# Second blocks of at most 64 tokens on column halves of the matmul array, in a hybrid decoder layer with a mixture of experts

## The chip, the cores and the metric

The kernel runs on one core of a Trainium2 chip. The metric is the device time of one execution in microseconds (us), the median of several runs. TensorE (PE) multiplies, VectorE (DVE) and ScalarE (ACT) do element-wise work, GpSimd (POOL) issues the gathers and scatters here, and SyncE (SP) issues the loads and stores. [...]

## What is computed

One decoder layer on 1024 tokens of width 1024 in float32: token mixing, then a mixture of experts, each with a residual and a layer norm. The change lies in the experts. A router picks for each token one of 4 groups and in it 2 of 8 experts, so 2048 assignments fall on 32 experts. Cut to that part, the reference is:

```python
def expert_block(args):
    xblk, e = args
    gu = xblk @ w_up[e]                      # 1024 -> 2 x 512
    return (jax.nn.silu(gu[:, :MOE_HIDDEN]) * gu[:, MOE_HIDDEN:]) @ w_down[e]   # 512 -> 1024
...
y = (yb.astype(jnp.float32) * pad_w[:, None]).astype(h.dtype)
out = jnp.zeros((t, d), h.dtype).at[pad_tok].add(y)
```

Each expert has its own `w_up` (4 MB) and `w_down` (2 MB); all 32 are read once.

## The kernel before

The mixing and the router take the first half of the time. The rest is the expert stage: 32 positions `e`, one expert each, in a loop written out at build time. The first four positions (`FIXED`) are experts 0 to 3. The others are sorted on the chip by their number of tokens and dealt out by a table (`place`, `reorder`): the largest four go to positions 5, 12, 19 and 26, the fifth to position 7. Those five (`BIG`) and the fixed four make up `TWO`, the positions that may have a second block of 128 tokens; anything beyond goes through a loop at the end that is skipped when nothing is left.

For each position a register `N[e]` holds (tokens + 127) / 16, rounded down. Branches on it choose the form. With N over 11 (more than 64 tokens) the first block runs whole; with N of 10 or 11 it is `parts(2)`, with at most 32 tokens `parts(4)`. In the whole form (`up_whole`, `down_whole`) the stationary operand is 128x128, the tokens of a block. In the parts (`up_parts`, `down_parts`) it is 64 or 32 columns wide, and the 2 or 4 matmuls that belong together write to different partitions of one PSUM bank, each with another slice of the weights. A float32 matmul leaves two records in the trace. With N over 15 (more than 128 tokens) there is a second block, which runs whole whatever its size: its up part goes to the PSUM tile `pup2` (named `ov` in the trace), `hidden` and `turn_hidden` make `eh2` of it, its down part goes to `pup2` again, and `result` weighs it into `yo2`, which a scatter adds to `xad` in DRAM. The scatters and gathers are cut to 16, 32, 48, 64 or 128 rows by `by_size`.

The weights come in tiles of 1 MB (two k of 128 rows) in the order `SEQ`: four up tiles of position e, then two down tiles of position e-1. `eload` issues a load on SP as soon as the code has released a tile, and the 19 tiles of the rings (`ring`, `pring` and the reused `more`, `gs`, `vn`, `y0a`, `y0b`, `y1a`, `uu`) are reused in turn. On each engine the order is the program's: for position e the first four k of up, the hidden layer of e-1 turned, the last four k of up, the tokens of e+1 turned, then down and finish of e-1. Every scatter to `xad` waits for the one before it to land, and at the end `xad` is read back for the last layer norm.

A branch on `N[e]` stands in the program of every engine that holds the register: TensorE, VectorE, and for positions of `TWO` ScalarE and GpSimd too, also where the engine has no work inside.

Of the kernel before, what the change touches and what calls it, by code (L numbers as in the profile page):

```python
# [59 lines left out]
def tile_hybrid_moe_layer(  # L60
# [1051 lines left out]
    ext = [pe.tile([P, 8, P], F32, name=f"ext{i}") for i in range(3)]  # L1112
# [4 lines left out]
    yo2 = pe.tile([P, 1024], F32, name="yo2")  # L1117
    N = {}
    TWO = [*range(FIXED), *BIG]
# [96 lines left out]
    def by_size(n, f, base=0):  # L1216
        with tc.If(n > base + 9) as some:
            with tc.If(n > base + 11) as many:
                f(slice(0, P))
            with many.Else():  # L1220
                with tc.If(n > base + 10) as more:
                    f(slice(0, 64))
                with more.Else():
                    f(slice(0, 48))
        with some.Else():
            with tc.If(n > base + 8) as more:
                f(slice(0, 32))
            with more.Else():
                f(slice(0, 16))
# [21 lines left out]
    eh, eh2 = (p4.tile([P, 4, P], F32, name=n) for n in ("eh", "eh2"))  # L1251
    wr, wr2 = ([p4.tile([P, 1], F32, name=f"{n}{i}") for i in range(m)] for n, m in (("wr", 2), ("wq", 3)))
# [46 lines left out]
    pup, pup2, pdn = (ps4.tile([P, 2, 512], F32, name=t) for t in ("up", "ov", "dn"))  # L1299
# [38 lines left out]
    def gate_up(w, m, j):  # L1338
        return w.rearrange("p (a b n) -> p a b n", a=2, b=m)[:, :, j]

    def up_whole(p, x, ks, w):
        for k in ks:
            for h in range(2):
                PE.matmul(p[:, h], x[:, k], gate_up(w[k], 2, h), start=k == 0, stop=k == 7)  # L1344

    def up_parts(m, p, x, ks, w):
        r = P // m
        o = p[:, 0].rearrange("p (a n) -> p a n", a=2)
        if m == 4:
            o = o[:, :, 0:256:2]  # L1350
        for k in ks:
            for j in range(m):
                c = gate_up(w[k], 2, j // 2)[:, :, j % 2:256:2] if m == 4 else gate_up(w[k], m, j)
                PE.matmul(o[j * r:(j + 1) * r], x[:, k, 0:r], c, start=k == 0, stop=k == 7)

    def down_whole(p, h, ks, w):
        for k in ks:
            for n in range(2):
                PE.matmul(p[:, n], h[:, k - 8], w[k][:, COLS[n]], start=k == 8, stop=k == 11)  # L1359

    def down_parts(m, p, h, ks, w):
        r, c = P // m, 4 // m
        for k in ks:
            j, i = divmod(k - 8, c)
            for q in range(m):
                PE.matmul(p[q * r:(q + 1) * r, 0, 0:D // m], h[:, i, j * r:(j + 1) * r],
                          w[k][:, q * (D // m):(q + 1) * (D // m)], start=k == 8, stop=k == 11)

    def by_parts(n, whole, parts):
        with tc.If(n > 9) as some:  # L1370
            with tc.If(n > 11) as many:
                whole()
            with many.Else():
                parts(2)
        with some.Else():
            parts(4)

    def up(e, ks, w):
        b = e % 2

        def whole():
            up_whole(pup, ext[b], ks, w)
            if e in TWO:
                with tc.If(N[e] > 15):
                    up_whole(pup2, ext[2], ks, w)

        by_parts(N[e], whole, lambda m: up_parts(m, pup, ext[b], ks, w))

    def down(e, ks, w):
        p = pd(e)  # L1390

        def whole():
            down_whole(p, eh, ks, w)
            if e in TWO:
                with tc.If(N[e] > 15):
                    down_whole(pup2, eh2, ks, w)

        by_parts(N[e], whole, lambda m: down_parts(m, p, eh, ks, w))

    def pd(e):  # L1400
        return pup2 if e == NE - 1 and e not in TWO else pdn
# [17 lines left out]
    def result(yo, p, w, m=1):  # L1419
        r, c = P // m, D // max(m, 2)  # L1420
        for n in range(max(m, 2)):
            rows, src = slice(0, r), (p[n * r:(n + 1) * r, 0, 0:c] if m > 1 else p[:, n])
            V.scalar_tensor_tensor(yo[rows, n * c:(n + 1) * c], src, w[rows], g2p[rows, n * c:(n + 1) * c],  # L1423
                                   op0=OP.mult, op1=OP.mult)

    def scatter(yo, tcol, rows):
        G.indirect_dma_start(out=xad, out_offset=bass.IndirectOffsetOnAxis(ap=tcol[rows], axis=0),  # L1427
                             in_=yo[rows], in_offset=None, bounds_check=T + P - 1, oob_is_err=True,
                             compute_op=OP.add)
# [17 lines left out]

    def finish_second(e):
        if e in TWO:
            with tc.If(N[e] > 15):  # L1450
                result(yo2, pup2, wr2[TWO.index(e) % 3])
                by_size(N[e], lambda rows: scatter(yo2, tokp[:, 1, e:e + 1], rows), 8)

    l2 = []
# [31 lines left out]
    def last_of(e):  # L1486
        down(e, range(8, 12), weights_of(e, range(8, 12)))
        release(e, range(8, 12))
        finish(e)
        finish_second(e)  # L1490

    for e in range(NE):
        up(e, range(4), weights_of(e, range(4)))
        release(e, range(4))
        if e == 0:
            reorder()
            ordered.append(True)
            while unused and len(RAW) < len(SEQ):
                eload()
        if e + 1 < NE:  # L1500
            count_all(e + 1)
            for x in (e + 1, e + 2):
                if x < NE and x == e + 1 + (x - 1 not in TWO):
                    gather_second(x)
        gather_weight(e, 0)
        if e:
            turn_hidden(act, eh)
            turn_hidden_second(e - 1)
        up(e, range(4, 8), weights_of(e, range(4, 8)))
        release(e, range(4, 8))  # L1510
        hidden(act, pup)
        hidden_second(e)
        turn_first(e + 1)
        if e:
            last_of(e - 1)
        if e + 1 < NE:
            turn_second(e + 1)
# [7 lines left out]
    with tc.If(most > 0):  # L1525
        free = list(unused)
        for e in range(NE):
            done = 1 + (e in TWO)
            ne = count(nbl, e, None, 8)
            with tc.If(ne > done):  # L1530
                x = e if e < FIXED else count(ordp, e, None, NE - 1)
                with tc.For_i(done, ne, 1) as j:
# [7 lines left out]
                    w = {}  # L1540
# [100 lines left out]
```

## Time and profile before

| | us |
|---|---|
| median of 3 runs | 1169.26 (1168.99 to 1174.07) |
| profiled execution | 1171.18 |
| its span, first to last instruction | 1169.3 |
| TensorE busy in the span | 1038.5 (89%) |
| VectorE, ScalarE, GpSimd busy | 553.8, 292.7, 358.9 |

The span is what the trace shows of the profiled execution; 1.9 us of its time lie around it. A busy TensorE is an account of issued matmuls, whose ends are modelled; it says nothing of how full the array is. The expert stage lies between about 570 and 1125 us of the span. In that stage the shares over the whole span don't help, since the stage has a stretch for each position with other sizes; it is read by stretches, by the waits in a stretch and by the order in time.

### The profile page before, as it was taken

The numbers are of one execution on the slowest core, as the hardware profiler recorded it, in microseconds if no ns is written. First come the engines' busy times: TensorE is split into PE (matmuls) and PEld (weight loads), VectorE is DVE, ScalarE is ACT, GpSimd is POOL, SyncE is SP. The second block draws the span as 40 slices with busy tenths as digits, with TensorE's granted clock in tenths as the row PEclk, the third lists the DMA queues.
The fourth block names the chain that finished last, engine by engine and source line by source line (L and its number), as shares of the span: only waits on it lengthen the run. The fifth ranks groups of instructions, "written<-read, shape, count | busy, mean of one in ns | idle before, by whom it ended". The sixth has DMA issues, their size and how long they took to land.

```text
span 1169.3 us, 16712 instructions
## 1 busy us (share of the span) xinstructions
PE 1038.5 (89%) x5758; PEld 687.5 (59%) x5758; DVE 553.8 (47%) x1018; ACT 292.7 (25%) x440; POOL 358.9 (31%) x271
## 2 busy tenths in 40 slices
PE   4999999899999989998678999899999999899920
PEld 3778888788788767777433454454444544454510
DVE  6858975737664489999511211130223113211338
ACT  3363326643224442221210110010011101110113
POOL 2325543262211236543412211231134113301225
PEclk9899999999999999999798999999999999899975
DMA  9954454444212325414999989999999999999964
GB/s 277 247 168 145 131 182 140 142 144 144 91 51 59 144 88 221 164 68 187 371 361 345 393 338 323 381 394 412 386 377 380 412 389 373 390 416 394 387 222 179
DMA packets 93631, 304.50 MB, mean 260 GB/s; under 512 B 14769, under 2 KB 42073, under 8 KB 68909
## 3 DMA queue, kind: packets, MB, share of 16 engines
q1 hardware_dynamic: 83900, 275.52, 63.4%
q0 software_dynamic: 8368, 22.90, 7.3%
q10 hardware_dynamic: 1216, 4.21, 0.9%
q8 instruction: 83, 1.36, 0.5%
q14 instruction: 64, 0.52, 0.1%
HBM read 281.09 MB, written 22.88 MB: 260 GB/s over the span
## 4 chain that ended last, share of the span: by engine, by line
PE 27%; DMA 25%; issue 25%; DVE 16%; ACT 3%; POOLq 1%; POOL 1%; SPq 1%; DVEq 0%; ACTq 0%
DMA xad<-yo,tokp 19%; DMA wr<-wd,aidp 4%; PE sm L302 4%; PE acc L623 3%; PE acc L625 3%; PE acc L624 3%; PE acc L621 2%; PE acc L619 2%; PE acc L620 2%; DVE y1a L234 1%; DMA wd<-w 1%; DVE pc L1022 1%; DVE Fg L886 1%; DMA xad<-Vv 1%; SPq L103 1%
## 5 line engine op out<-in xcount | busy, mean ns | idle before, releaser
L1406 DVE TENSOR_TENSOR act<-up,act 128x512 f32<-128x512 f32 x32 | 22.1, 692 | 299.7 <-ACT act L1405 244.3
L1427 POOL DMA_INDIRECT xad<-yo,tokp x36 | 52.9, 1470 | 231.7 <-DVE yo L1423 106.1
L1423 DVE SCALAR_TENSOR_TENSOR yo<-dn,wr,g2p 32x256 f32<-32x256 f32 (+2 forms) x94 | 52.1, 563 | 126.9 <-PE ov L1359 39.0
L1412 ACT ACTIVATE eh<-tp 128x512 f32<-128x512 f32 x36 | 21.1, 596 | 315.5 <-PE tp L1411 274.8
L623 PE MATMUL acc<-whi,hTh 128*128 128x512 f32 x192 | 83.1, 433 | 0.0
L1212 POOL DMA_INDIRECT KS<-h2d,tokp x32 | 30.6, 958 | 164.0 <-PE tp L1319 155.1
L166 ACT ACTIVATE whi<-wr 128x1024 fp32r<-128x1024 f32 (+1 forms) x44 | 44.9, 1021 | 128.1 <-PE acc L625 67.9
L625 PE MATMUL acc<-whi,hTl 128*128 128x512 f32 x192 | 76.0, 396 | 0.0
L624 PE MATMUL acc<-wlo,hTh 128*128 128x512 f32 x192 | 75.4, 393 | 0.0
L167 POOL TENSOR_TENSOR wlo<-wr,whi 128x1024 fp32r<-128x1024 f32 (+1 forms) x15 | 35.8, 2385 | 119.9 <-ACT whi L166 108.3
L302 PEld LDWEIGHTS sm<-QP,KS 128*128 128x128 f32 x448 | 58.2, 192 | 7.3 <-issue 3.3
L619 PE MATMUL acc<-hTh,whi 128*128 128x512 f32 x144 | 59.3, 411 | 0.0
L302 PE MATMUL sm<-QP,KS 128*128 128x64 f32 x448 | 56.1, 269 | 2.6 <-DVE KS L315 1.6
L1344 PE MATMUL up<-pring,ext 128*128 128x512 f32 x128 | 56.7, 593 | 1.6 <-DVE yo L1423 1.6
L621 PE MATMUL acc<-hTh,wlo 128*128 128x512 f32 x144 | 56.9, 395 | 0.5 <-DVE wlo L167 0.3
L881 PE MATMUL pa<-wh,yl 128*128 128x512 f32 (+1 forms) x128 | 51.8, 405 | 5.5 <-DVE yl L865 5.5
L620 PE MATMUL acc<-hTl,whi 128*128 128x512 f32 x144 | 56.7, 393 | 0.0
L880 PE MATMUL pa<-wl,yh 128*128 128x512 f32 (+1 forms) x128 | 51.3, 401 | 4.7 <-DVE wl L1052 4.7
L879 PE MATMUL pa<-wh,yh 128*128 128x512 f32 (+1 forms) x128 | 53.4, 417 | 1.5 <-ACT wh L1051 0.9
L1405 ACT ACTIVATE act<-up 128x512 f32<-128x512 f32 x32 | 19.1, 597 | 135.2 <-PE ov L1344 52.3
L443 POOL TENSOR_TENSOR vec<-vec,y1a 128x1024 f32<-128x1024 f32 x14 | 35.4, 2527 | 55.2 <-ACT y1a L442 55.2
L167 DVE TENSOR_TENSOR wlo<-wr,whi 128x1024 fp32r<-128x1024 f32 (+1 forms) x29 | 38.4, 1324 | 22.6 <-ACT whi L166 21.9
(476 smaller groups left out, 2243.2 us busy)
## 6 DMA issues: line engine op xcount, KB each, us to landing
pring<-in_w_up SPq DMA_DIRECT2D x52, 1024.0 KB, 20.5
pring<-in_w_down SPq DMA_DIRECT2D x28, 1024.0 KB, 8.5
ring<-in_w_up SPq DMA_DIRECT2D x28, 1024.0 KB, 16.4
wr<-in_w_in SPq DMA_DIRECT2D x44, 512.0 KB, 6.0
y1a<-in_w_ada SPq DMA_DIRECT2D x32, 512.0 KB, 4.0
ring<-in_w_down SPq DMA_DIRECT2D x12, 1024.0 KB, 20.4
y0a<-in_w_up SPq DMA_DIRECT2D x8, 1024.0 KB, 15.1
y0b<-in_w_up SPq DMA_DIRECT2D x8, 1024.0 KB, 24.3
```

The costliest lines, as they stand in the source:

```text
L167: (G if u % 3 == 2 and u > W8 else V).tensor_tensor(lo, w, hi, op=OP.subtract)
L302: PE.matmul(p[:, hd], chd(KS)[:, c4, hd], chd(QP)[:, c4, hd].rearrange("p (b two i) -> p b two i", two=2, i=h)[:, :, 1, :], start=True, st ...
L619: PE.matmul(a[i], hi[:, j, sl], hTh[k], start=st, stop=False)
L620: PE.matmul(a[i], hi[:, j, sl], hTl[k], start=False, stop=False)
L621: PE.matmul(a[i], lo[:, j, sl], hTh[k], start=False, stop=sp)
L623: PE.matmul(a[i], hTh[k][:, sl], hi[:, j], start=st, stop=False)
L624: PE.matmul(a[i], hTh[k][:, sl], lo[:, j], start=False, stop=False)
L625: PE.matmul(a[i], hTl[k][:, sl], hi[:, j], start=False, stop=sp)
L879: PE.matmul(p, yh[:, k], wh[k][:, sl], start=k == 0, stop=False)
L1344: PE.matmul(p[:, h], x[:, k], gate_up(w[k], 2, h), start=k == 0, stop=k == 7)
L1423: V.scalar_tensor_tensor(yo[rows, n * c:(n + 1) * c], src, w[rows], g2p[rows, n * c:(n + 1) * c], op0=OP.mult, op1=OP.mult)
L1427: G.indirect_dma_start(out=xad, out_offset=bass.IndirectOffsetOnAxis(ap=tcol[rows], axis=0), in_=yo[rows], in_offset=None, bounds_check=T ...
```

## The change

Where a position has a second block (N over 15), its size is looked at too. With N over 19 (more than 64 tokens in the second block) all stays as it was. Otherwise its up and down matmuls use the form `parts(2)`, 64 stationary columns and two column halves, and `result` reads the halves from one bank. `hidden`, `turn_hidden`, gather and scatter are unchanged. The finish of a second block now has two branches, one for `result` and one for the scatter.

```diff
+    def second_by_size(n, whole, halved):
+        with tc.If(n > 15):
+            with tc.If(n > 19) as many:
+                whole()
+            with many.Else():
+                halved()
...
             if e in TWO:
-                with tc.If(N[e] > 15):
-                    up_whole(pup2, ext[2], ks, w)
+                second_by_size(N[e], lambda: up_whole(pup2, ext[2], ks, w),
+                               lambda: up_parts(2, pup2, ext[2], ks, w))
...
             if e in TWO:
-                with tc.If(N[e] > 15):
-                    down_whole(pup2, eh2, ks, w)
+                second_by_size(N[e], lambda: down_whole(pup2, eh2, ks, w),
+                               lambda: down_parts(2, pup2, eh2, ks, w))
...
     def finish_second(e):
         if e in TWO:
+            second_by_size(N[e], lambda: result(yo2, pup2, wr2[TWO.index(e) % 3]),
+                           lambda: result(yo2, pup2, wr2[TWO.index(e) % 3], 2))
             with tc.If(N[e] > 15):
-                result(yo2, pup2, wr2[TWO.index(e) % 3])
                 by_size(N[e], lambda rows: scatter(yo2, tokp[:, 1, e:e + 1], rows), 8)
```

The first place is TensorE at position 26, the last four k of the up part (`ov` is the second block's tile, `ext_4022` its turned tokens, `y0b` and `y1a` the weight tiles; lines with - are of before, with + of after, and the line numbers of after are higher by up to 8).

```order
 L1344 MATMUL up<-y0b,ext_4020 128x512 x4
 L1344 MATMUL up<-y1a,ext_4020 128x512 x4
-L1384 COMPARE_AND_BRANCH
+L1379 COMPARE_AND_BRANCH
+L1380 COMPARE_AND_BRANCH
 L1344 MATMUL ov<-y0b,ext_4022 128x512 x4
 L1344 MATMUL ov<-y1a,ext_4022 128x512 x4
-L1384 UNCONDITIONAL_BRANCH x2
+L1380 UNCONDITIONAL_BRANCH
+L1354 MATMUL ov<-y0b,ext_4022 64x512 x4
+L1354 MATMUL ov<-y1a,ext_4022 64x512 x4
```

One more comparison stands ahead of the second block, and a second body with 64 columns stands behind the whole one; the matmuls of the first block and their order are untouched. TensorE's listing has 3981 rows before and 4152 after.

The second place is VectorE at the finish of the same position, before (`wq_4238` holds the weights of the second block's tokens, `yo_4039` is `yo2`):

```order
1554 L1217 UNCONDITIONAL_BRANCH
1555 L1450 COMPARE_AND_BRANCH
1556 L1423 SCALAR_TENSOR_TENSOR yo_4039<-ov,wq_4238,g2p 128x512 x2
1557 L1217 COMPARE_AND_BRANCH
1558 L1218 COMPARE_AND_BRANCH
```

And the same place after:

```order
1656 L1217 UNCONDITIONAL_BRANCH
1657 L1379 COMPARE_AND_BRANCH
1658 L1380 COMPARE_AND_BRANCH
1659 L1430 SCALAR_TENSOR_TENSOR yo_4039<-ov,wq_4238,g2p 128x512 x2
1660 L1380 UNCONDITIONAL_BRANCH
1661 L1430 SCALAR_TENSOR_TENSOR yo_4039<-ov,wq_4238,g2p 64x512 x2
1662 L1380 UNCONDITIONAL_BRANCH
1663 L1379 UNCONDITIONAL_BRANCH
1664 L1459 COMPARE_AND_BRANCH
1665 L1217 COMPARE_AND_BRANCH
```

The one test at L1450 has become a pair of tests around the result and a test of its own (L1459) around the scatter, which stands in the other engines' programs at this place too.

## Rows read from the trace of the kernel before

**Rows 1.** Stretches: length, busy us (count) of PE, PEld, DVE, ACT, POOL; clock, DMA share, GB/s.
```profile
660.00:690.00 30.00, 30.00 (x83) 13.93 (x79) 2.19 (x3) 1.20 (x3) 2.45 (x2) 1.00 0.89 356
...
1020.00:1050.00 30.00, 30.00 (x137) 14.59 (x136) 3.80 (x7) 2.17 (x4) 1.76 (x2) 1.00 1.02 418
1050.00:1080.00 30.00, 30.00 (x112) 14.54 (x112) 4.01 (x6) 2.88 (x5) 4.95 (x4) 1.00 1.02 388
1080.00:1110.00 30.00, 30.00 (x247) 15.02 (x246) 9.04 (x16) 4.67 (x8) 8.56 (x7) 1.00 1.02 390
```

**Rows 2.** Waits of SP's queue, 1020 to 1104: us in total, times, longest.
```profile
SPq L103 <- DMA pring<-in_w_up: 19.2, 9, 3.2
...
SPq L103 <- PE tp L1319: 0.8, 3, 0.3
```

**Rows 3.** The same view, 660 to 700 us.
```profile
SPq L103 <- PE ov L1344: 26.9, 4, 10.9
```

**Rows 4.** GpSimd in order of time: start, us taken, instruction, [idle before, releaser].
```profile
851.53 1.57 POOL L1427 DMA_INDIRECT xad<-yo,tokp  x1 [9.87 <-DMA xad<-yo,tokp]
...
963.75 1.58 POOL L1427 DMA_INDIRECT xad<-yo,tokp  x1 [10.28 <-DMA xad<-yo,tokp]
...
1080.73 1.44 POOL L1427 DMA_INDIRECT xad<-yo,tokp  x1 [9.47 <-DMA xad<-yo,tokp]
```

**Rows 5.** TensorE in order of time at position 26 (x: records merged into a row).
```profile
1023.82 3.60 PE L1344 MATMUL ov<-vn,ext 128*128 128x512 f32 x8
...
1030.69 0.63 PE L1411 MATMUL tp<-ident,act 128*128 128x128 f32 x4
...
1060.64 7.03 PE L1359 MATMUL ov<-pring,eh 128*128 128x512 f32 x16
1067.50 3.60 PE L1344 MATMUL up<-pring,ext 128*128 128x512 f32 x8
```

**Rows 6.** TensorE in order of time, into and out of position 30's 64-column form.
```profile
1093.54 3.60 PE L1359 MATMUL dn<-uu,eh 128*128 128x512 f32 x8
1097.06 3.65 PE L1354 MATMUL up<-pring,ext 128*64 128x512 f32 x16
1100.65 0.74 PE L1411 MATMUL tp<-ident,act 128*128 128x128 f32 x4
```

**Rows 7.** Issues on SP's queue in order of time: position 31's up, the last weight tile.
```profile
1077.36 4.04 SPq L103 DMA_DIRECT2D pring<-in_w_up  x2
...
1098.17 0.33 SPq L103 DMA_DIRECT2D gs<-in_w_down  x1
```

**Rows 8.** DMA issues, 1020 to 1104: count, KB each, median us to landing.
```profile
pring<-in_w_up SPq DMA_DIRECT2D x8, 1024.0 KB, 21.6
```

**Rows 9.** TensorE in order of time, positions 30 and 31 at the end.
```profile
1107.82 2.01 PE L1354 MATMUL up<-pring,ext 128*32 128x256 f32 x32
...
1115.63 1.94 PE L1366 MATMUL dn<-ring,eh 128*64 128x512 f32 x8 [0.22 <-DMA ring<-in_w_down]
...
1120.78 1.07 PE L1366 MATMUL ov<-gs,eh 128*32 128x256 f32 x16 [0.72 <-DMA gs<-in_w_down]
```

**Rows 10.** TensorE at position 0's down; then the finish branch: count, ns least/median/most.
```profile
612.04 1.93 PE L1366 MATMUL dn<-pring,eh 128*32 128x256 f32 x16 [3.33 <-issue]
...
L1450 PEldq COMPARE_BRANCH  x9: 73/208/223, 612.5 to 1060.6; - x9
```

**Rows 11.** Stretches of 5 us as in rows 1, and TensorE in them.
```profile
1005.00:1010.00 5.00, 1.83 (x24) 0.88 (x28) 0.00 (x0) 0.00 (x0) 0.00 (x0) 0.80 1.04 347
1010.00:1015.00 5.00, 5.00 (x42) 2.71 (x37) 1.38 (x2) 1.19 (x2) 0.99 (x1) 0.52 1.01 424
...
1009.28 1.93 PE L1354 MATMUL up<-ring,ext 128*32 128x256 f32 x16 [2.56 <-DMA ring<-in_w_up]
```

**Rows 12.** GpSimd in order of time, the last two scatters.
```profile
1119.48 1.40 POOL L1427 DMA_INDIRECT xad<-yo,tokp  x1 [6.09 <-DVE yo L1423]
...
1125.52 1.31 POOL L1427 DMA_INDIRECT xad<-yo,tokp  x1 [4.64 <-issue]
```

## Prediction, made before the change was timed

> **What bounds the kernel now.** I read the stretches first: busy time by engine, granted clock and DMA share in 30 us pieces [rows 1]. From 1020 to 1110 us two things are full at once. TensorE is busy 30.00 of 30.00 us, and the DMA engines show a share of 1.02 at 388 to 418 GB/s. A busy PE alone says little, so the next view is what the queue that issues the weight loads (SP's) waited for. Between 1020 and 1104 us its longest entry is a wait on earlier loads, 19.2 us, and the largest one on TensorE is 0.8 us [rows 2]. A free buffer is therefore nearly always there, and loads are issued as fast as the DMA engines drain them. Around the first large expert (660 to 700 us) it is the other way about: SP waited 26.9 us on TensorE's second-block matmuls [rows 3], and the DMA share of 660 to 690 us is 0.89 [rows 1]. So TensorE sets the pace early in the expert stage, and the weight stream sets it at the end. The question is where the change acts.
>
> **Where it acts.** The reference's router, evaluated on its own inputs, sends 241, 238, 228 and 188 tokens to its four largest experts and at most 127 to any other. Second blocks are what exceeds 128: 113, 110, 100 and 60 tokens. Only the last has at most 64. The planner puts the ranks behind the four fixed experts at positions 5, 12, 19 and 26, so that one is position 26. The trace agrees. The second scatters took 1.57 and 1.58 us to issue at positions 12 and 19 (1.58 at position 5 too) and 1.44 us at position 26 [rows 4], as a scatter of fewer rows would. The second block's matmuls there run between 1023.82 and 1067.50 us [rows 5], inside the stretch where the loads set the pace.
>
> **The matmuls, part by part.** Its second block has three pieces on TensorE: up over the first four k, up over the last four, and down. Each is 16 records of 128x512, 0.43 us apart: the first piece with its twin tile runs from 1023.82 to 1030.69, 6.87 us, and the down piece at 1060.64 has the same form and 7.03 us [rows 5]. Three pieces make 20.6 us. The 64-column form of such a piece is in the trace as position 30's first block: 16 records from 1097.06 to 1100.65, 3.59 us instead of 6.87 [rows 6]. Two matmuls on different column halves thus run at once. Changing the form costs a little: eight pairs of 0.43 would be 3.44, so 0.15 us goes on leaving the form, and entering it took 1097.06 less 1093.54 less 3.44, or 0.08 [rows 6]. Three pieces in the new form are 3 x (3.59 + 0.08) = 11.0 us, so TensorE saves **9.6 us** at position 26.
>
> [...]
>
> **What of it reaches the end.** TensorE leaves position 26 at 1067.50 [rows 5]; after, about 9.6 us earlier. It then runs on tiles that are already there until it meets the loads. For the up tiles of position 31, SP issued the first at 1077.36 [rows 7], and a load landed 21.6 us later in the median [rows 8], so at about 1099.0 (an estimate). TensorE started there at 1107.82 [rows 9], 8.8 us later. An advance of 9.6 us exceeds that: TensorE waits from there on, tile by tile. The last two experts' down tiles were met without slack already: at 1115.63 and 1120.78 TensorE waited 0.22 and 0.72 us for the load [rows 9], the latter issued at 1098.17 [rows 7]. So the saving on the path is **0**, hidden behind the stream of loads. The ends of this term: a gain of 0.8 us, if all of SP's largest wait on TensorE falls away, and no loss from the matmuls themselves.
>
> **Branches and code.** A taken second block now decodes one more compare at each of four sites, and every one of the nine positions that can have a second block tests twice at the finish instead of once. On TensorE's sequencer such a compare took 208 ns in the median [rows 10]. Nine positions by 0.21 us is 1.9 us in all. At the four fixed positions the sequencer is not always ahead (TensorE stood idle before 612.04 without a releaser [rows 10]), so I count those four, 0.8 us, and take half, **+0.4**. From position 5 on TensorE works without a gap behind its sequencer [rows 1], or waits for loads, and these branches are covered; uncovered, they would cost the 1.9. The new 64-column bodies also lengthen TensorE's program by 171 rows of the listing. What that does to instruction supply the trace doesn't price directly. The nearest row is 612.04: TensorE stood 3.33 us, for nothing that the profile shows, between two tiles of one down step [rows 10]. I take 0, as most jumps show no such gap, and keep 3.3 us to either side, since moved code could add such a gap or remove it.
>
> **The clock at the tail.** [...] Whether the clock has recovered by then is open; 0 to +1.7, and I take half, **+0.8**.
>
> **The sum.** 0 + 0.4 + 0.8 = +1.2 us. The profiled execution lasted 1171.18 us (span 1169.3 and 1.9 around it), 1.9 above the median of 1169.26; on it the sum gives 1172.4, and on the median **1170.5**.
>
> **Rivals.**
> *TensorE sets the pace to the end* (faster). For it: PE is busy 30.00 of 30.00 [rows 1], so no load came late to it between 1020 and 1110. If the loads could follow, the full 9.6 us would be gained: 1159.7. Against it: the DMA share of 1.02, SP's waits, and the two waits at 1115.63 and 1120.78. Chance 0.05.
> *The longer program starves TensorE* (slower). Jumps over the new bodies could stop its sequencer for 3.3 us each, as at 612.04. That decides only where TensorE is late: before and at position 5, where SP waited 26.9 us on it, or behind the last load. One stall gives 1173.8, two give 1177.1. For it: such gaps exist already among the fixed positions. Against it: at position 5 TensorE worked 30.00 of 30.00 us from 660 to 690 [rows 1], with queued matmuls to cover a late sequencer. Chance 0.13, of which 0.05 for two or more.
> *The clock stays low to the last matmul* (slower, little): 1169.26 + 0.4 + 1.7 = 1171.4. Chance 0.08. [...]
> *The change doesn't act*, because no second block falls to the new form: 1169.7. The 1.44 us scatter and the token counts speak against it. Chance 0.04.
>
> **How the numbers follow.** The forecast has the remaining 0.70. A difference of 0.5%, 5.8 us, is about what a measurement of this kernel can tell from no change. Faster than 1163.4 is only the first rival, 0.05. Slower than 1175.1 is two stalls, 0.05, and I add 0.02 for an unlucky sum of one stall and the low clock. The rest, 0.88, is no change. The range goes from one stall fewer, 1169.26 - 3.3, or 1166, to one stall with both small terms at full size, 1169.26 + 3.3 + 0.8 + 1.7, or 1175.
>
> **What would show it.** In the changed kernel's trace, position 26 should have 48 second-block records of 128x64 in pairs, its three pieces near 3.6 us, and TensorE near 1058 where it stood at 1067.50. SP's issue times from 1020 on should hardly move, and the DMA share stay near 1.02. New waits of TensorE on loads should stand at position 31's up tiles, with the granted clock low in part of 1100 to 1120, and the last two scatters within 2 us of 1119.48 and 1125.52. If the last weight load were issued several us before 1098, the prediction would be wrong: then TensorE was holding the loads back. A last load on time with a late end would point to the tail.

## The result and the profile after

The changed kernel took 1178.64 us in the median (1173.2 to 1182.27, 17 runs); the kernel before, run beside it, 1171.41 us (1168.99 to 1174.07, 17 runs). The ratio is 1.0065 with a 95% interval of [1.0054, 1.0076]: slower by about 7.6 us, where 1.2 us were forecast and the range ended at 1175. (Of the 8.1 us between the forecast of 1170.5 and the measured median, 2.2 are the base: the kernel before had 1169.26 in its first three runs and 1171.41 here.) The change does what it says at position 26 and gains nothing there. The time is lost some 400 us earlier, in positions 0 to 4, where not one matmul was changed.

The profiled execution of the changed kernel lasted 1179.19 us. First its page: span, busy time by engine, and the queue q8, one of the two that the page marks as bringing instructions (packets, MB, share of 16 engines).

```profile
span 1177.5 us, 16828 instructions
...
PE 1032.9 (88%) x5758; PEld 682.3 (58%) x5758; DVE 554.4 (47%) x1018; ACT 292.9 (25%) x440; POOL 359.0 (30%) x271
...
q8 instruction: 87, 1.43, 0.5%
```

TensorE is busy 5.6 us less than before (1038.5), and the span is 8.2 us longer: it idled more. Queue q8 carried 83 packets (1.36 MB) before and 87 now; 1.43 MB by 87 is 16.4 KB a packet.

**The saving is there.** TensorE in order of time at position 26, to be held against [rows 5] (start, us taken, instruction, records):

```profile
1032.42 1.94 PE L1354 MATMUL ov<-vn,ext 128*64 128x512 f32 x8
...
1036.01 0.74 PE L1418 MATMUL tp<-ident,act 128*128 128x128 f32 x4
...
1063.08 3.65 PE L1366 MATMUL ov<-pring,eh 128*64 128x512 f32 x16
1066.67 3.70 PE L1344 MATMUL up<-pring,ext 128*128 128x512 f32 x8
```

A piece takes 3.59 us (1032.42 to 1036.01, 1063.08 to 1066.67), as [rows 6] promised, where it took 6.87 and 7.0. TensorE leaves the position at 1066.67, 0.8 us ahead of [rows 5], although by then the whole program ran some 8 us late.

**It ends in waits for loads.** TensorE in order of time at the end, to be held against [rows 9]. In brackets stand the idle time before and what ended it; a q behind an engine's name is its sequencer, and "issue" means that the engine waited for nothing that the profile shows:

```profile
1108.57 1.07 PE L1366 MATMUL dn<-pring,eh 128*32 128x256 f32 x16 [1.63 <-DMA pring<-in_w_down]
1111.24 1.93 PE L1354 MATMUL up<-pring,ext 128*32 128x256 f32 x16 [1.60 <-DVE yo L1430]
...
1119.26 1.11 PE L1354 MATMUL up<-ring,ext 128*32 128x256 f32 x16 [1.17 <-DMA ring<-in_w_up]
1121.45 1.94 PE L1366 MATMUL dn<-ring,eh 128*64 128x512 f32 x8 [1.08 <-DMA ring<-in_w_down]
1123.93 1.94 PE L1366 MATMUL dn<-ring,eh 128*64 128x512 f32 x8 [0.54 <-DMA ring<-in_w_down]
```

In most of these rows TensorE waits for its load, 0.54 to 1.63 us each, where the first wait for a load in [rows 9] was 0.22 us. The last weight load (`gs<-in_w_down`) was issued at 1108.99, against 1098.17 in [rows 7], 10.8 us later: the loads themselves are late.

**Where the time went.** I matched SP's loads of the two kernels one by one; their order is the same. The lag of the changed kernel is 7.8 us at the load that before was issued at 596.19, 3.7 at 613, 5.2 from 623 to 634, 3.9 to 4.2 from 639 to 653 and 7.4 to 7.7 at 655 to 661. From there it varies between 5.7 and 11.1 us and is 8.1 when `xad` is read back. So 7.7 us of it are made before position 5's matmuls begin (661.85 before, 669.53 after), and at the end nothing of that has been recovered. TensorE in this stretch, the changed kernel:

```profile
584.90 0.63 PE L1354 MATMUL up<-y0a,ext 128*32 128x256 f32 x6
590.09 1.91 PE L1354 MATMUL up<-y0a,ext 128*32 128x256 f32 x10 [4.56 <-issue]
591.94 1.98 PE L1319 MATMUL tp<-ident,KS 128*128 128x128 f32 x8
594.87 5.54 PE L1344 MATMUL up<-y0b,ext 128*128 128x512 f32 x8 [0.95 <-DMA more<-in_w_up]
600.25 3.60 PE L1344 MATMUL up<-y1a,ext 128*128 128x512 f32 x8
...
615.31 1.93 PE L1366 MATMUL dn<-pring,eh 128*32 128x256 f32 x32
620.77 3.65 PE L1354 MATMUL up<-pring,ext 128*64 128x512 f32 x16 [3.53 <-DVEq L1332]
...
627.03 3.65 PE L1354 MATMUL up<-pring,ext 128*64 128x512 f32 x16 [1.93 <-issue]
...
660.32 1.93 PE L1354 MATMUL up<-y1a,ext 128*32 128x256 f32 x16 [2.57 <-issue]
```

And the same work in the kernel before:

```profile
584.46 1.08 PE L1354 MATMUL up<-y0a,ext 128*32 128x256 f32 x16
585.48 1.22 PE L1319 MATMUL tp<-ident,KS 128*128 128x128 f32 x8
588.45 0.67 PE L1344 MATMUL up<-y0b,ext 128*128 128x512 f32 x1 [1.74 <-DVEq L1440]
589.47 3.16 PE L1344 MATMUL up<-y0b,ext 128*128 128x512 f32 x7 [0.35 <-issue]
592.47 3.60 PE L1344 MATMUL up<-y1a,ext 128*128 128x512 f32 x8
```

The telling row is 590.09. A tile's 16 records, straight code without a branch and with the weights already there, are cut into 6 and 10, with 4.56 us of nothing between; the kernel before ran all 16 at once. The pause costs more than its length: behind it 10 records take 1.91 us where 16 took 1.08, the transposes 1.98 instead of 1.22, and the next tile 5.54 instead of some 3.7. By `y1a` TensorE is 7.8 us late (600.25 against 592.47), where it was 0.4 us late at the start of `y0a`. The granted clock, which the profile gives as a share of full speed, goes with it (columns as in [rows 1]; changed kernel):

```profile
585.00:590.00 5.00, 0.53 (x10) 0.84 1.01 419
590.00:595.00 5.00, 3.95 (x19) 0.50 1.09 254
595.00:600.00 5.00, 5.00 (x8) 0.64 0.99 383
```

Only PE is listed in these rows. TensorE stood from 585.5 to 590.1 and came back at a granted clock of 0.50, and 0.64 from 595 to 600, where the kernel before had 1.00 from 585 to 600. The lag shrinks to 3.7 us at 613 because the stall of [rows 10], 3.33 us at 612.04, doesn't occur in the changed kernel, and it grows again with the pauses before 620.77, 627.03 and 660.32.

What arrives in or at such a pause is an instruction packet. The DMA traffic from 584 to 591 us of the changed kernel, by queue:

```profile
q1 hardware_dynamic: 815, 2.77, 99.4%
q8 instruction: 1, 0.02, 0.8%
q14 instruction: 1, 0.01, 0.3%
```

The packet of q8 starts at 587.60 us and takes 0.89; TensorE goes on 1.60 us after its end. Those at 618.15, 624.31 and 657.60 end 1.69, 1.51 and 1.58 us before TensorE goes on at 620.77, 627.03 and 660.32. The same holds beyond this kernel: in all kept traces of this case, 17 pauses of 1.3 us or more that the profile marks "issue" lie between 578 and 680 us, and each ends 1.2 to 2.8 us after the end of a q8 packet. (A shorter one doesn't: 1.15 us before 604.99, with no packet's end in the 7 us ahead of it.) The packet of q14 doesn't fit: it starts at 590.09, when TensorE goes on. But from 575 to 672 us the kernel before has 11 packets of q8 and the changed one 12, and most are followed by no pause; the traces don't say for which engine a packet is. By the page a packet of q8 has 16.4 KB in the mean; what asks for one, and whether a packet that comes late causes the pauses here, no run shows by itself.

### The profile page after: what moved, and what is told of

The parts are those of the page before. It is cut to its first block, busy times and chain, and to the rows that moved or that the text cites. A ratio compares the mean times of both kernels' runs of the same rounds, so it can differ in the third digit from the quotient of the medians.

```text
span 1177.5 us, 16828 instructions
## 1 busy us (share of the span) xinstructions
PE 1032.9 (88%) x5758; PEld 682.3 (58%) x5758; DVE 554.4 (47%) x1018; ACT 292.9 (25%) x440; POOL 359.0 (30%) x271
## 3 DMA queue, kind: packets, MB, share of 16 engines
q8 instruction: 87, 1.43, 0.5%
## 4 chain that ended last, share of the span: by engine, by line
DMA 29%; PE 27%; issue 22%; DVE 15%; ACT 3%; POOLq 1%; SPq 1%; POOL 1%; DVEq 0%; ACTq 0%
DMA xad<-yo,tokp 21%; PE sm L302 4%; PE acc L623 3%; PE acc L625 3%; PE acc L624 3%; DMA wr<-wd,aidp 2%; DMA xad<-Vv 2%; DMA KS<-h2d,tokp 2%; PE acc L621 2%; PE acc L619 2%; PE acc L620 2%; DVE y1a L234 1%; DVE pc L1022 1%; DVE Fg L886 1%; PE pa L881 1%
## 5 line engine op out<-in xcount | busy, mean ns | idle before, releaser
L1354 PE MATMUL up<-pring,ext 128*32 128x256 f32 (+1 forms) x512 | 45.6, 432 | 9.1 <-DVEq L1332 3.5
```

## The experiments

Theory A, a guess at the mechanism: the bodies that the change adds, and which most positions only jump over, shift TensorE's program, so that instruction fetches fall on other places; in positions 0 to 4, where TensorE isn't ahead, some of these places stall it. Theory B: the half form at position 26 itself, or the clock at the tail, costs the time. Theory C: the added tests cost it, some time each. A fourth, D, has the fixed positions paced by their loads, so that nothing at TensorE could matter there.

**The form never runs, the code stays.** `e1_half_never` is the changed kernel with the inner test always true:

```diff
-            with tc.If(n > 19) as many:
+            with tc.If(n > 15) as many:
```

> The changed kernel with one number altered: the second test asks n > 15 again, so the half form is in the program at all nine positions but never runs; position 26's second block is whole, as before the change. Theory A (the longer TensorE program moves instruction fetches to places in positions 0 to 4 where TensorE is not ahead): as slow as the changed kernel, 1178 to 1180 us, loads issued 7 to 8 us late from position 5 on, the same two or three gaps without a releaser (near 585, 625 and 658 us). Theory B (the half form at position 26 or its clock at the tail costs the time): back to 1171 to 1172. Theory C (the added tests cost a little each): 1178, but with the delay growing at every one of the nine positions instead of in jumps.

Measured: 1179.39 us against 1171.65, ratio 1.0061 [1.0041, 1.0081]. The whole loss is there without a single half-form matmul, so B falls. The cut stands at the same record, 6 ahead of it and 10 behind (TensorE in order of time):

```profile
589.30 1.91 PE L1354 MATMUL up<-y0a,ext 128*32 128x256 f32 x10 [4.29 <-issue]
```

**The change position by position.** Three kernels give the new form to some positions and leave the others as before: position 26 alone, the fixed positions 0 to 3 alone (where no second block exists, so only tests and code are added), and the five of `BIG` alone. In each, `second_by_size` and the finish take the position too, with `e == BIG[-1]`, `e < FIXED` or `e >= FIXED`:

```diff
-    def second_by_size(n, whole, halved):
+    def second_by_size(e, n, whole, halved):
         with tc.If(n > 15):
-            with tc.If(n > 19) as many:
+            if e == BIG[-1]:
+                with tc.If(n > 19) as many:
+                    whole()
+                with many.Else():
+                    halved()
+            else:
                 whole()
-            with many.Else():
-                halved()
```

> The half form and its tests at position 26 alone; the other eight positions have the old code, so TensorE's program is 19 listing rows longer instead of 171, all of it behind position 25. Theory A: positions 0 to 25 as before the change, and the 9 us that TensorE saves at position 26 hidden behind the loads: 1170 to 1173 us, ratio 0.999 to 1.002. Theory B: all of the loss stays, 1178. Theory C: one ninth of the loss, 1172.

> The half form and its tests at positions 0 to 3 alone, none of which has a second block in this data; nothing runs in the half form. Theory A: TensorE's program up to position 3 is that of the changed kernel, so the gaps there are the same: loads late by 7 to 8 us at position 5, 1177 to 1180 us. Theory B: 1171. Theory C: four ninths of the loss, 1174 to 1175, spread over the four positions.

> The half form and its tests at positions 5, 7, 12, 19 and 26, the fixed four with the old code. Theory A: the fixed positions as before the change, loads at position 5 no more than 1 us late, and later the loads set the pace: 1170 to 1173 us. Theory B: 1178. Theory C: five ninths, 1175.

Measured: position 26 alone 1171.48 us, ratio 0.9995 [0.9982, 1.0008]; fixed positions alone 1177.60 us, 1.0052 [1.0035, 1.0068]; `BIG` alone 1172.05 us, 1.0003 [0.999, 1.0017]. The loss belongs to the four positions in which the half form never runs and only one more test, at the finish, does. What was added there puts the cut where the changed kernel has it (`e3_only_fixed`):

```profile
590.42 1.91 PE L1354 MATMUL up<-y0a,ext 128*32 128x256 f32 x10 [4.83 <-issue]
```

C falls for this pause by the order in time. The changed kernel's added tests are the one of the size (L1380) and the one around the scatter (L1459). On the engine that meets each first they ran so (count, ns least/median/max, first and last start):

```profile
L1380 PEldq COMPARE_BRANCH  x32: 65/175/389, 669.4 to 1064.4; - x32
...
L1459 ACTq COMPARE_BRANCH  x9: 34/45/50, 615.4 to 1057.0; - x9
```

TensorE stopped at 585.5, and the load issued at 603.97 was 7.8 us late, before any engine had met either test. Up to there the two programs run the same instructions; what differs is code that is jumped over or lies further on.

With position 26 alone the stretch is that of the kernel before (`e2_only_26`):

```profile
588.38 3.92 PE L1344 MATMUL up<-y0b,ext 128*128 128x512 f32 x8 [1.74 <-DVEq L1450]
...
611.42 1.37 PE L1366 MATMUL dn<-pring,eh 128*32 128x256 f32 x16 [3.05 <-issue]
```

**Less code than before.** `e5_big_two_before` is the kernel before, with the second-block branches taken out of the four fixed positions. An expert there with over 128 tokens would go through the loop at the end; on these inputs none has. `e6_big_two_26` adds the half form at position 26 to it.

```diff
-    for e in (slice(0, FIXED), *(slice(b, b + 1) for b in BIG)):
+    for e in (slice(b, b + 1) for b in BIG):
...
-    TWO = [*range(FIXED), *BIG]
+    TWO = [*BIG]
```

> The kernel before with second blocks provided for at positions 5, 7, 12, 19 and 26 only (TWO and the limit table without the fixed four, which have none in this data; a second block there would go to the loop at the end). TensorE's program is 109 listing rows shorter, most of it ahead of position 4. Theory A (instruction fetches met in positions 0 to 4 set when position 5 starts): fewer of them and fewer waits at the branches, position 5 starts 3 to 8 us earlier, 1164 to 1169 us. Rival D (the fixed positions are paced by the loads, DMA share about 1.0 there): within 1 us of before, 1171 to 1172.

> The same, and the half form at position 26 alone. Theory A with the saving of position 26 hidden behind the loads: the same time as e5_big_two_before within 1 us. If an earlier start lets TensorE set the pace at the end, the half form would add up to 9.6 us of gain on top; if the low clock at the tail costs time, it is up to 2 us slower than e5_big_two_before.

Measured: 1160.74 us, ratio 0.9928 [0.9911, 0.9945], and 1161.21 us, 0.9925 [0.9899, 0.9952], against 1169.97. More was gained than expected, and both beat the two kernels of this case. These kernels leave out tests and waits at branches as well as code, so the gain doesn't tell one from the other: of the pauses over 0.6 us of before that are gone, only the one of [rows 10] is marked "issue", and others (2.31 us before 635.80, 1.21 before 606.52) ended at another engine's sequencer. The half form adds nothing that can be told from zero, as the prediction has it. D falls: TensorE was busy 81.13 us of the 97 from 575 to 672 before, 74.23 after the change and 92.79 here. From 575 to 655 us `e5_big_two_before` has no pause longer than the two below (TensorE in order of time):

```profile
576.72 1.20 PE L1319 MATMUL tp<-ident,KS 128*128 128x128 f32 x8 [2.22 <-issue]
...
588.39 3.67 PE L1344 MATMUL up<-y0b,ext 128*128 128x512 f32 x8 [1.74 <-ACT ext L1323]
```

Position 5's second block starts at 651.3 us, 17.4 us earlier than before, and 8.4 us of that reach the end. The waits of SP's queue from 640 to 700 us in `e5_big_two_before` (us in total, times, longest) show what stops the rest, beside the 26.9 us that it waited on the same matmuls before [rows 3]:

```profile
SPq L103 <- DMA ring<-in_w_up: 11.8, 4, 3.3
...
SPq L103 <- PE ov L1344: 5.9, 2, 3.0
```

The loads now wait for earlier loads: here the weight stream is the bound.

**Code that is never executed.** If the place of the code decides, then code that nobody runs must move the time. Extra copies of a whole up body go into a branch that position 0 doesn't take; 2 copies are 64 TensorE instructions (8 matmuls each, with two weight loads and two matmul records for one), 8 copies 256. Theory A has two forms here: the place of the code decides, or the length of the program. First on the kernel before:

```diff
                 with tc.If(N[e] > 15):
+                    for _ in range(2 if e == 0 and ks[0] == 0 else 0):
+                        up_whole(pup2, ext[2], ks, w)
                     up_whole(pup2, ext[2], ks, w)
```

> The kernel before with the whole second-block body of position 0's first up step written three times instead of once. The body is never executed (position 0 has 23 tokens); no branch and no wait is added, only 64 more matmul and weight-load instructions, which the program jumps over. The changed kernel has the same number of additional instructions ahead of position 0's second up step. Theory A: TensorE stands 4 to 5 us in the middle of up<-y0a near 585.5 us, as in the changed kernel, where the kernel before has no gap, and a load waits behind it; the time moves by over 2 us, either way at the end since later fetches move too. Rival C (tests and waits): nothing moves, 1171 to 1172 us.

> [...] In the form that the length of the program decides: slower than e7_dead_4k, 1176 to 1184. Rival C: 1171 to 1172 with nothing moved.

Measured: 1167.58 us, ratio 0.9977 [0.9965, 0.9989], and 1165.94 us, 0.9966 [0.9955, 0.9977]. The time of `e7_dead_4k` moved by over 2 us, as theory A had it, but no pause appeared at `y0a`, and that was a miss. `e8_dead_16k` has no pause at `y0a` either, and A's form by length (1176 to 1184) was a miss: the time came out 1.6 us below that of `e7_dead_4k`. The gap of [rows 10] is gone in both kernels; the same 32 records run through (first `e7_dead_4k`):

```profile
607.43 1.93 PE L1366 MATMUL dn<-pring,eh 128*32 128x256 f32 x32
```

and `e8_dead_16k`, where a small new cut stands in an earlier tile:

```profile
580.72 1.86 PE L1354 MATMUL up<-gs,ext 128*32 128x256 f32 x10 [0.70 <-issue]
...
610.09 1.93 PE L1366 MATMUL dn<-pring,eh 128*32 128x256 f32 x32
```

So a longer program is not slower as such, and the time moves with no test added. The same edit on the changed kernel was to tell place from length once more:

```diff
-                second_by_size(N[e], lambda: up_whole(pup2, ext[2], ks, w),
+                second_by_size(N[e], lambda: [up_whole(pup2, ext[2], ks, w)
+                                              for _ in range(3 if e == 0 and ks[0] == 0 else 1)],
```

> The changed kernel with two extra copies of the whole up body, 64 TensorE instructions that are never executed, in the branch of position 0's first up that isn't taken; the work is the changed kernel's. If the loss hangs on where the fetches of the program fall (theory A): one or more of the changed kernel's three long pauses (4.56 us at the narrow up of position 0, 1.93 us near 627, 2.57 us near 660) goes or moves, and the time comes out at 1166 to 1176 us although the program is longer. If what counts is the length alone: the pauses stay and grow, 1179 to 1182 us. If the tests or the half form cost the time, nothing moves: 1178 to 1179.5 us.

> As the run with two extra copies, but eight of them, 256 TensorE instructions that are never executed. Theory A: the pauses stand elsewhere than in the changed kernel, 1164 to 1176 us, with no promise that it lies between the others. Length alone: above the run with two copies, 1182 to 1190 us. Tests or half form: 1178 to 1179.5 us.

Measured: with 64 instructions more 1175.0 us, ratio to the kernel before 1.0036 [1.0024, 1.0048], about 3.4 us better than the changed kernel; with 256 more 1183.1 us, 1.0104 [1.0085, 1.0124]. The first is as A has it: `y0a` runs uncut, and pauses show at other places, of 1.1 to 1.5 us each (`e9_after_dead_4k`):

```profile
585.04 1.71 PE L1354 MATMUL up<-y0a,ext 128*32 128x256 f32 x16
...
613.04 0.63 PE L1366 MATMUL dn<-pring,eh 128*32 128x256 f32 x6 [1.11 <-issue]
...
620.14 0.71 PE L1419 MATMUL tp<-ident,act 128*128 128x128 f32 x4 [1.47 <-issue]
```

The second missed A's range and lies in that of length alone. But length alone would have made the first slower too, and the rows tell more (`e10_after_dead_16k`):

```profile
579.42 1.49 PE L1354 MATMUL up<-more,ext 128*32 128x256 f32 x10 [2.45 <-issue]
...
587.45 1.06 PE L1354 MATMUL up<-y0a,ext 128*32 128x256 f32 x5
592.77 1.92 PE L1354 MATMUL up<-y0a,ext 128*32 128x256 f32 x11 [4.25 <-issue]
...
623.91 6.21 PE L1354 MATMUL up<-pring,ext 128*64 128x512 f32 x16 [3.73 <-issue]
...
665.47 1.11 PE L1354 MATMUL up<-y1a,ext 128*32 128x256 f32 x16 [1.65 <-issue]
```

With 256 instructions put ahead of it, the cut in `y0a` is back, one record from where the changed kernel has it (5 and 11 instead of 6 and 10), and three of the pauses behind it stand at the same tiles (623.91 for 620.77, 665.47 for 660.32; the one of 1.93 us at 627.03 is down to 0.91). One more cut, 2.45 us, has come in front. With 64 instructions the cut was gone. A period of 256 instructions would fit this pair, but that is a guess that no run shows, and it doesn't explain the pair on the kernel before: there 256 more instructions should have brought the gap of [rows 10] back, and did not.

## Why the prediction was wrong

- **Where it acts, and the 9.6 us at TensorE: right.** Only position 26 changed form, at 3.59 us a piece.
- **Zero of it on the path: right.** Position 26 alone gave 0.9995, and `e6_big_two_26` stands at 1161.21 beside 1160.74 without the half form. The first leaves room for -2.1 to +0.9 us, the second pair for some 4 us either way. The waits on loads came at the tail, as forecast.
- **Branches, +0.4: not told apart.** The added tests on the five big positions, with the half form at position 26, came to 1.0003 [0.999, 1.0017], -1.2 to +2.0 us; for the fixed positions tests and code come together.
- **Code, 0 with 3.3 us to either side: the step that failed.** It measured +7.6 us. Three things were wrong in it. The price of one stall was read as its idle time. [rows 10] held more: 612.04 took 1.93 us for 16 records, and 16 of that size run in 1.07 at a granted clock of 1.00 ([rows 9], 1120.78); here the granted clock was 0.70 from 610 to 615 us and 0.62 from 615 to 620. The next tile in the kernel before was slow too:

```profile
614.80 5.64 PE L1354 MATMUL up<-pring,ext 128*64 128x512 f32 x16 [0.83 <-DMA uu<-in_w_up]
```

  The same work takes 3.65 us at 621.82, so that stall had cost 3.33 + 0.86 + 1.99, or 6.2 us at TensorE. Behind the 4.56 us pause the slow clock (0.50 and 0.64) cost some 3.8 us more (1.91, 1.98 and 5.54 us for work of 0.7, 1.2 and 3.7). The number of stalls was bounded at one, with no row behind that bound: the trace of before had 11 packets of q8 from 575 to 672 us, and in the changed kernel four pauses came while one went. And "most jumps show no such gap" counted jumps; by the packets beside the pauses, those of q8 should have been counted.
- **The rival named it.** "The longer program starves TensorE" had the added code and the place, positions before 5, and its two stalls gave 1177.1, near the 1178.64 measured. That number is luck: it priced a stall at 3.3 us, where the one pause at `y0a` set TensorE back by over 7 (from 0.4 to 7.8), and the three others and the stall that went nearly cancel. Its chance of 0.13 leaned on the cover at position 5. That cover held: TensorE was busy 30.00 of 30.00 us from 667 to 697 after the change too. But it says nothing of positions 0 to 4, and I had not read SP's waits there. In the kernel before, from 575 to 668 us, SP's queue waited mostly for TensorE and for branches of its sequencer (us in total, times, longest):

```profile
SPq L103 <- PE up L1354: 20.2, 9, 4.4
...
SPq L103 <- PEq L1384: 13.4, 2, 8.1
```

  L1384 is the test for a second block. The changed kernel's test from 575 to 676 us:

```profile
SPq L103 <- PEq L1379: 26.9, 3, 11.1
```

  So TensorE was mostly the late one there, and what it loses goes to the end: the condition that the rival named was met, and this view would have shown it.
- **The clock at the tail, +0.8: the fall came, the cost did not.** The changed kernel's stretches (columns as in [rows 1]):

```profile
1110.00:1115.00 5.00, 3.25 (x32) 1.25 (x32) 1.62 (x4) 0.00 (x0) 2.38 (x2) 0.56 1.01 423
1115.00:1120.00 5.00, 3.83 (x44) 1.65 (x36) 0.00 (x0) 0.60 (x1) 0.00 (x0) 0.75 1.00 398
1120.00:1125.00 5.00, 3.38 (x22) 1.06 (x16) 0.69 (x1) 0.60 (x1) 0.00 (x0) 1.00 0.79 330
```

No run shows the +0.8, or the 1.7 of which it is half. The kernel before had a slow row of this kind (16 records in 1.93 us, the clock at 0.80 and then 0.52 [rows 11]), and at the tail of the changed kernel the clock fell to 0.56. But from 1120 to 1125 us it was back at 1.00, and position 30's last down tile took 1.94 us at 1123.93, as in [rows 9]. The last two scatters start at 1127.78 and 1133.12, 8.3 and 7.6 us behind [rows 12]: the lag of the loads and nothing more.

What stays open is how a place in the program becomes a stall. That what was added at the fixed positions causes the loss is shown, and for the first 7.8 us of lag, at `y0a`, that none of the added instructions had run by then. That the pauses are instruction fetches is argued, not shown: it rests on the packets that end 1.2 to 2.8 us before TensorE goes on, on the cuts in straight code and on the runs with code that nobody executes. Which packets, if any, come too late was not derived, and `e8_dead_16k` contradicts a plain period of 256 instructions.

## What to carry to other kernels

Code in a branch that is never taken was not free here, where TensorE was the late one: look in the trace for a pause without a releaser inside one tile's records, and price it with the slow clock behind it (0.50 and 0.64 after the pause of 4.56 us). Before adding a form to every position, add it only where it can run; the same edit at position 26 alone cost nothing, and taking unused branches out of the first four positions gained 0.7%, where the form brought nothing. This stage, bound by loads at its end, still lost for good what TensorE lost at its start: every load from position 5 on was issued 5.7 us late or more.

## What the hardware showed unexpectedly

A pause of 4.56 us in front of 10 records of a tile put TensorE over 7 us further behind two tiles on (0.4 to 7.8 us), as the clock came back at 0.50 and was at 1.00 only after 600 us. In the stretch from 578 to 680 us of all kept traces, each of the 17 pauses of TensorE of 1.3 us or more that the profile marks "issue" ended 1.2 to 2.8 us after the end of an instruction packet of q8. Instructions that are never executed moved the time both ways: 64 of them by -0.23% on the kernel before and by about -0.3% on the changed one, 256 by -0.34% and +0.4%.
